# Two-layer hybrid block on one core: retention through a running state, norm factors spread by fp32r products, and side work started at other places

## The chip, the core and the metric

The kernel runs on one core of a Trainium2 chip. Its five engines are TensorE (PE, matrix products; PEld in the profile is its weight load), VectorE (DVE), ScalarE (ACT), GpSimd (POOL) and SyncE (SP, which here only issues DMAs). Each engine carries out its own instructions in the order in which the program lists them, and waits at an instruction until the data and buffers it needs are there. The metric is device time of one launch in microseconds (us); smaller is better.

## The reference, cut to what matters

Two layers, 512 tokens (S), width 1024 (D), four heads of 128 in each of three branches, feed-forward width 2816. Everything is float32.

```python
def retention(q, k, v):                      # CHUNK = 64
    q = rotary(q, pos); k = rotary(k, pos) * dk ** -0.5
    log_g = log1p(-exp2(-5.0 - arange(h)))   # one decay per head
    d_intra = exp(abs(idx[:, None] - idx[None, :]) * log_g)
    scores = einsum('bnihd,bnjhd->bnhij', qc, kc) * d_intra
    o_intra = einsum('bnhij,bnjhe->bnihe', scores, vc)
    kv = einsum('bnjhd,bnjhe->nbhde', kc * k_w, vc)
    _, r_prev = lax.scan(lambda r, kv_n: (g_chunk * r + kv_n, r), 0, kv)
    return o_intra + einsum('bnihd,nbhde->bnihe', qc * q_w, r_prev)

def hybrid_layer(x, ...):
    h = modulate(rms_norm(x, norm1_g), shift1, scale1)
    rq, rk, rv, rg, gq, gk, gv, glr, gg, fq, fk, fv, ff = split(h @ w_in)
    ret = silu(rg) * head_group_norm(retention(rq, rk, rv))
    gla_o = silu(gg) * rms_norm(gla(gq, gk, gv, log_a))
    fox_o = forgetting_attention(rms_norm(fq), rms_norm(fk), fv, ff + b_fox_f)
    mixed = sum(sigmoid(h @ w_mg + b_mg) * (branches @ w_br)) @ w_o
    x = x + gate1 * mixed
    h2 = modulate(rms_norm(x, norm2_g), shift2, scale2)
    u, g = split(h2 @ w_up)
    return x + gate2 * ((silu(causal_dwconv(u)) * g) @ w_down)
```

## The kernel before

**The big projections.** Activations lie as eight 128x512 tiles (`h[kc]`, features down the partitions, tokens along). Weights come in units of 128x1024. A unit is loaded by SP's queue (`wr`), its upper half is cast by ACT (`wh`, L175), the rest is subtracted by DVE (`wl`, L184), and every product is made of three one-pass fp32r products (`mm3`, L295 to L297: wh with hhi, wh with hlo, wl with hhi). `ahead()` prepares the units some steps ahead. A `col_block` is one output tile of 128x512: 8 x 3 = 24 such products. `head_group` (L428) is the first stage after a norm, where the inputs `h[kc]` are still being made: by `h_a` and `h_b` (DVE `ht`, ACT `hhi`, DVE `hlo`), tile by tile. At the start of the kernel it runs on eight banks with whole 512-column tiles. In the three later places (`half`: before layer 0's feed-forward, before layer 1's projections, before layer 1's feed-forward) it runs on six banks and takes each of its 8 tiles in two halves of 256 columns, so that the first half of the tokens starts before the norm of the second half is known.

**The norm.** `Norm.sums` (L346) makes the sum of squares per token by products with a column of ones (`nrm`), DVE makes v, POOL the power -1/2 (`r`, L352). `Norm.spread` (L354) multiplies r, broadcast, by the identity (float32, L356), which puts the factor of each token on all partitions (`nrmb`); ACT copies it to `rb`.

**After the head group of a layer.** The token group (L697 to L699, 276 columns; `tok_group`) makes the columns that are needed token by token. On ACT and DVE it is accompanied by `t_sum` and `t_low` (L598 to L617: sums and differences of the tiles of h for the paired projections, `ta`, `tb` and their casts `tah`, `tbh`, `tal`, `tbl`). Then the `col_block`s of the forgetting attention's q and k, the retention's v, the gates and so on follow.

**Side work.** What lies between the projections is written as generators: `qk_norm` (the norm of fq and fk: ACT squares `qsq` L544, cast `qsh`, DVE `qsl`, two products `qn` with ones L549 and L550), `gates_item` (forget gates: transposes, elementwise steps, a scan L741, transposes `cumc` L745, a DMA on POOL's queue), `la_item`, `fox_item` (L803, L819), `kv_item`, `ret_item`, `gla_item`. They wait in `queue` and are advanced by `tick()`, which each `col_block` calls twice. A tick lets every active item take one elementwise phase (`yield E_`) and then one phase on PE (`yield P1`, `P2`: with so many of the NA = 3 banks of the pool `psa`). An item in the queue starts when the counter `cool` has run down; each tick lowers it by one, and a started item sets it again by the second number with which it was queued. The order of all engines is thus fixed when the program is built.

**Retention.** Per head four items, `ret_item(hh, jb)`, one for each key block jb. Each makes the scores of its 128 keys against all later queries (L942: 512, 384, 256, 128 columns, float32), DVE multiplies by the decay table `dec` and PE adds up `ro` (L954, 1, 2, 3 and 4 products of 128 columns). The four decay tables are loaded by SP's queue at one place ahead of the first item. The four items of a head follow each other with `cool` 1.

**The start.** Ten warm-up products on the tile `warm` (W0), five (W1) and again ten (W2) fill PE while x, c and the first weights come in; between them the squares of x and the Silu of c are made.

A bank is a PSUM tile, and a slot is one of the NSLOT = 65 tiles of 128x512 that all side work shares.

Of the kernel before, what the change touches and what calls it, by code (L numbers as in the profile page):

```python
# [19 lines left out]
W0, W1, W2 = 10, 5, 10  # L20
# [6 lines left out]
NH = 4  # L27
# [19 lines left out]
for _n, _w in (("ident", 128), ("suf", 128), ("mask", 128), ("ind", 2),  # L47
               ("eps", 1), ("heps", 1), ("one", 1), ("mhalf", 1)):
    CC[_n] = (_o, _w)
    _o += _w  # L50
# [38 lines left out]
def tile_hybrid_layers(ctx: ExitStack, tc: tile.TileContext, xT, cvec, wall, wada, par, a2, cst, tabs, out):  # L89
# [45 lines left out]
    ones = const.tile([128, 128], F32, tag="ones", name="ones")  # L135
    onesr = const.tile([128, 128], F32R, tag="onesr", name="onesr")
# [200 lines left out]
    class Norm:  # L337
        def __init__(self, acc):
            self.acc = acc
            self.ps = bm("nrm")  # L340
            self.pb = bm("nrmb")
            self.rb = slot("rb")
            self.v = sm_p.tile([128, 4], F32, tag="v", name="v")
            self.r = sm_p.tile([128, 4], F32, tag="r", name="r")

        def sums(self, b0, b1):  # L346
# [5 lines left out]
            G.tensor_tensor(r, v, cc("mhalf").to_broadcast([128, b1 - b0]), op=ALU.pow)  # L352
# [60 lines left out]
    def head_group(l, sec, nm, h, half):  # L413
# [6 lines left out]
        def mms(kc, hf, bs=range(GB)):  # L420
# [5 lines left out]
            for n, (wi, hi) in enumerate(((0, 0), (1, 0), (0, 1))):  # L426
                for f in fl:
                    T.matmul(banks[f % GB][:, ts], lhsT=got[f // 8][wi][:, (f % 8) * 128:(f % 8) * 128 + 128],  # L428
                                 rhs=h[kc][hi][:, ts], start=kc == 0 and hf != 1 and n == 0,
                                 stop=kc == KD - 1 and n == 2, skip_group_check=hf is not None)  # L430
# [25 lines left out]
        else:  # L456
            hq = [(1, 0), (2, 0), (3, 0), (0, 1), (1, 1)]
            for kc in range(2, KD):
                hq += [(kc + 2, 0)] * (kc + 2 < KD) + [(kc, 1)]
            hp = []  # L460

            def hc(n=1):
                for _ in range(n):
                    if hq:
                        kc, hf = hq.pop(0)
                        hp.append((kc, hf, h_a(l, sec, kc, nm.rb, h, HS[hf])))
                    if hp and (len(hp) > 1 or not hq):
                        kc, hf, t = hp.pop(0)
                        h_b(l, sec, kc, t, h, HS[hf])
# [6 lines left out]
            hc()  # L476
# [5 lines left out]
            for kc in range(KD):  # L482
                hc()
                mms(kc, 1)
                hc()
                ahead()
                if kc + 3 < KD:
                    mms(kc + 3, 0)
# [48 lines left out]
    def layer(l, nm, h):  # L537
# [46 lines left out]
        cool[0] = 10 if l else 6  # L584
# [134 lines left out]
        def gates_item():  # L719
# [21 lines left out]
            V.tensor_tensor_scan(cum[0:4], e[0:4], m[0:4], 0.0, op0=ALU.mult, op1=ALU.add)  # L741
            yield P1
# [195 lines left out]
        def ret_item(hh, jb):  # L938
            w = S - jb * 128
            yield ("p", 1, lambda: [("rq", hh) in R, ("rk", hh) in R, ("rv", NB - 1) in R, ("dec", hh) in R])  # L940
            ps = ba("rs")
            T.matmul(ps[:, 0:w], lhsT=R["rk", hh][:, jb * 128:jb * 128 + 128], rhs=R["rq", hh][:, jb * 128:S],  # L942
                     start=True, stop=True)
# [5 lines left out]
            yield P0 if jb else P1
            if jb == 0:  # L950
                R["ro", hh] = ba("ro")
            po = R["ro", hh]
            for j in range(jb + 1):
                T.matmul(po[:, jb * 128:jb * 128 + 128],  # L954
                         lhsT=R["rP", hh, j][:, (jb - j) * 128:(jb - j) * 128 + 128],
                         rhs=R["rv", j][:, hh * 128:hh * 128 + 128], start=j == 0, stop=j == jb)
            if jb < NB - 1:
                return
# [59 lines left out]
        for i in range(4):  # L1018
            col_block(h, rot_evac("rk", i))
        for hh in range(NH):  # L1020
            R["dec", hh] = slot("dec")
            Q.dma_start(out=R["dec", hh], in_=tabs[2 + hh])
        for hh in range(NH):
            for jb in range(NB):
                queue.append((ret_item(hh, jb), 1))
# [174 lines left out]
    with tc.manual_schedule():  # L1200
# [20 lines left out]

        pc = [bm("cb"), bm("cb")]
# [184 lines left out]
```

## Time and profile before

| what | value |
|---|---|
| time, median of 3 runs | 1830.86 us (1830.72 to 1831.59) |
| the profiled execution, its time | 1827.52 us |
| its span, first to last instruction | 1825.8 us |
| mean granted TensorE clock | 0.996 |
| HBM read | 237.41 MB, 132 GB/s over the span |
| time of the packets of the hardware DMA queue, as a share of 16 engines' span | 36.1% |
| POOL busy | 128.4 us, 7% |
| ACT waiting for PE before a weight cast | 204.2 us in 62 waits |

A row of the timeline is: start, duration, engine, line, operation, output<-inputs, shapes, count; in brackets the idle time of the engine just before, and what ended it. A group row has busy time, mean duration in ns, then the idle time before its instructions. A row of the windows is: the stretch, its length, then busy time of PE, PEld, DVE, ACT and POOL with the counts, the granted clock of PE, the busy share of the DMA engines and their GB/s. Matmuls are pipelined and their ends are modelled, so the distance of two starts tells what a product costs, not its listed duration. A float32 product leaves two matmul records, an fp32r product and a transpose one.

### The profile page before, as it was taken

The page shows a single profiled execution, that of the slowest core. Times are in us where ns is not written, and L with a number is a line of the kernel's source. Part 1 is how long each engine was busy: PE and PEld are TensorE (multiplying, and loading weights), DVE is VectorE, ACT ScalarE, POOL GpSimd, SP SyncE. Part 2 cuts the span into 40 slices and gives each one's busy share as a digit, 9 for nine tenths or more (in the row PEclk, how much of TensorE's full clock was granted, in tenths as well). Part 3 has the DMA queues.
Part 4 walks back from the last instruction along what each step waited for, and adds up shares of the span by engine and source line. Part 5 has one row for each costly group of instructions (what it writes and reads, how often), then busy time and mean ns, then how long its engine had stood idle before and what let it go on. Part 6 is the DMA issues. An engine that isn't in the chain of part 4 may idle for free.

```text
span 1825.8 us, 22697 instructions
## 1 busy us (share of the span) xinstructions
PE 1786.8 (98%) x8895; PEld 1486.4 (81%) x8895; DVE 1059.9 (58%) x1643; ACT 715.8 (39%) x1192; POOL 128.4 (7%) x152
## 2 busy tenths in 40 slices
PE   9998999999999999999999989999999999999999
PEld 6776878888889888888898767788888898888887
DVE  7876674675666776754257767745444466445321
ACT  4577533432324433332146765334223244333220
POOL 3222010100000000000001210101000000000000
PEclk9999999999999999999999999999999999999999
DMA  9477332356452565554324762322422223232131
GB/s 358 127 170 174 104 104 81 127 185 221 160 173 93 166 217 198 199 196 166 98 76 108 204 152 80 116 69 76 144 93 92 81 93 115 93 103 94 47 124 48
DMA packets 72519, 243.11 MB, mean 133 GB/s; under 512 B 8232, under 2 KB 8658, under 8 KB 72412
## 3 DMA queue, kind: packets, MB, share of 16 engines
q1 hardware_dynamic: 66444, 220.67, 36.1%
q0 software_dynamic: 5968, 20.99, 5.9%
q8 instruction: 70, 1.15, 0.3%
q14 instruction: 37, 0.30, 0.1%
HBM read 237.41 MB, written 4.21 MB: 132 GB/s over the span
## 4 chain that ended last, share of the span: by engine, by line
PE 83%; DVE 8%; ACT 5%; issue 2%; POOL 1%; DMA 0%; SPq 0%; POOLq 0%; ACTq 0%; DVEq 0%
PE bm L295 22%; PE bm L297 22%; PE bm L296 22%; PE bm L428 4%; PE ga L428 4%; DVE wl L184 2%; ACT wh L175 2%; PE bm L647 1%; PE bm L651 1%; PE bm L649 1%; PE ro L954 1%; PE rs L942 1%; DVE fl L809 1%; DVE qsl L531 1%; POOL qsq L557 1%
## 5 line engine op out<-in xcount | busy, mean ns | idle before, releaser
L184 DVE TENSOR_TENSOR wl<-wr,wh 128x1024 fp32r<-128x1024 f32 x326 | 397.5, 1222 | 296.2 <-ACT wh L175 294.3
L295 PE MATMUL bm<-hhi,wh 128*128 128x512 f32 x1232 | 494.9, 402 | 0.0
L297 PE MATMUL bm<-hhi,wl 128*128 128x512 f32 x1232 | 480.9, 390 | 0.0
L296 PE MATMUL bm<-hlo,wh 128*128 128x512 f32 x1232 | 480.5, 390 | 0.0
L175 ACT CAST wh<-wr 128x1024 fp32r<-128x1024 f32 x326 | 338.6, 1046 | 304.1 <-PE bm L296 204.2
L295 PEld LDWEIGHTS bm<-hhi,wh 128*128 128x128 f32 x1232 | 231.7, 188 | 52.8 <-issue 5.3
L296 PEld LDWEIGHTS bm<-hlo,wh 128*128 128x128 f32 x1232 | 231.9, 188 | 50.6 <-issue 2.9
L297 PEld LDWEIGHTS bm<-hhi,wl 128*128 128x128 f32 x1232 | 231.7, 188 | 49.5
L295 PE MATMUL bm<-fah,wh 128*128 128x512 f32 (+1 forms) x374 | 141.0, 377 | 0.0
L296 PE MATMUL bm<-fal,wh 128*128 128x512 f32 (+1 forms) x374 | 140.8, 377 | 0.0
L297 PE MATMUL bm<-fah,wl 128*128 128x512 f32 (+1 forms) x374 | 140.8, 377 | 0.0
L205 DVE SCALAR_TENSOR_TENSOR ar<-ar,cact 128x1024 f32<-128x1024 f32 x80 | 97.4, 1217 | 0.0
L1090 DVE SCALAR_TENSOR_TENSOR x<-bm,mod,x 128x512 f32<-128x512 f32 (+1 forms) x39 | 25.5, 655 | 101.5 <-PE bm L297 101.5
L295 PEld LDWEIGHTS bm<-fah,wh 128*128 128x128 f32 x374 | 70.4, 188 | 13.0
L297 PEld LDWEIGHTS bm<-fah,wl 128*128 128x128 f32 x374 | 70.4, 188 | 13.0
L296 PEld LDWEIGHTS bm<-fal,wh 128*128 128x128 f32 x374 | 70.4, 188 | 12.7
L1127 ACT ACTIVATE fu<-fu 128x512 f32<-128x512 f32 x44 | 27.8, 632 | 102.9 <-DVE fu L1125 102.8
L1128 DVE TENSOR_TENSOR fu<-fu,bm 128x512 f32<-128x512 f32 x42 | 28.9, 688 | 65.3 <-PE bm L297 53.9
L334 ACT ACTIVATE sq<-x 128x512 f32<-128x512 f32 (+1 forms) x35 | 19.0, 545 | 104.1 <-DVE x L1090 103.0
L1050 ACT ACTIVATE mg<-bm,der 128x512 f32<-128x512 f32 x48 | 33.0, 688 | 65.2 <-PE bm L297 65.2
L295 PE MATMUL bm<-mxh,wh 128*128 128x256 f32 (+1 forms) x176 | 58.6, 333 | 0.0
L296 PE MATMUL bm<-mxl,wh 128*128 128x256 f32 (+1 forms) x176 | 58.3, 331 | 0.0
(256 smaller groups left out, 2718.6 us busy)
## 6 DMA issues: line engine op xcount, KB each, us to landing
wr<-wall SPq DMA_DIRECT2D x302, 512.0 KB, 3.8
ar<-wada SPq DMA_DIRECT2D x80, 512.0 KB, 4.7
wr<-wall POOLq DMA_DIRECT2D x32, 512.0 KB, 6.1
ad<-wada SPq DMA_DIRECT2D x32, 256.0 KB, 6.2
x<-xT SPq DMA_DIRECT2D x16, 256.0 KB, 4.8
cumb<-cumd POOLq DMA_DIRECT2D x8, 256.0 KB, 7.4
dec<-tabs SPq DMA_DIRECT2D x8, 256.0 KB, 2.7
x<-xs SPq DMA_DIRECT2D x8, 256.0 KB, 5.4
```

Source lines behind the costliest of these rows:

```text
L175: A.copy(hi, raw[plan[i][1]])
L184: V.tensor_tensor(lo, raw[plan[i][1]], hi.bitcast(F32), op=ALU.subtract)
L205: V.scalar_tensor_tensor(out=r, in0=r, scalar=1.0, in1=cact, op0=ALU.mult, op1=ALU.mult, accum_out=mod[l][:, b:b + 1])
L295: T.matmul(o, lhsT=wh, rhs=ah, start=first, stop=False)
L296: T.matmul(o, lhsT=wh, rhs=al, start=False, stop=False)
L297: T.matmul(o, lhsT=wl, rhs=ah, start=False, stop=last)
L334: A.activation(t[:, ts], x[k][:, ts], AF.Square)
L428: T.matmul(banks[f % GB][:, ts], lhsT=got[f // 8][wi][:, (f % 8) * 128:(f % 8) * 128 + 128], rhs=h[kc][hi][:, ts], start=kc == 0 and hf != ...
L1050: A.activation(g, o, AF.Tanh, scale=0.5, bias=der[l][:, i * 8 + j:i * 8 + j + 1])
L1090: V.scalar_tensor_tensor(out=x[j][:, ts], in0=o[:, ts], scalar=mod[l][:, sec * 8 + j:sec * 8 + j + 1], in1=x[j][:, ts], op0=ALU.mult, op1= ...
L1127: A.activation(t, t, AF.Silu)
L1128: V.tensor_tensor(t, t, pg, op=ALU.mult)
```

## The change

1. The warm-up at the start is shorter (W0 10 to 8, W2 10 to 4), and the two Silu of c come after all squares of x.
2. `Norm.spread`: r is split into rh and rl (two small DVE operations in `sums`), and two fp32r products with the identity take the place of one float32 product.
3. `head_group`, half form: the tiles 0 to 2 still go in halves, the tiles 3 to 7 as whole 512 columns.
4. `cool` after the head group is 4 (layer 0) and 8 (layer 1), before 6 and 10: `qk_norm` starts two ticks earlier.
5. `gates_item` has one more `yield E_` between the scan and its transposes.
6. Retention: one item per head. Scores within a block of 128 only (4 products of 128 columns), keys turned token by token (3 transposes, `rkT`), weighted by ACT with the column `kdec` (`rkw`), 3 products with v (`rkv`), a running state of three blocks (`rst`: one ACT copy, two DVE operations), queries times decay (`rqd`), and 4 + 3 products for `ro`. Items follow each other with `cool` 4. The decay tables are loaded one head at a time, in the item of the head before.
7. One slot fewer (64).

```diff
-W0, W1, W2 = 10, 5, 10
+W0, W1, W2 = 8, 5, 4
...
@@ Norm.sums
             G.tensor_tensor(r, v, cc("mhalf").to_broadcast([128, b1 - b0]), op=ALU.pow)
+            V.tensor_copy(self.rh[:, b0:b1], r)
+            V.tensor_tensor(self.rl[:, b0:b1], r, self.rh[:, b0:b1].bitcast(F32), op=ALU.subtract)
@@ Norm.spread
-                T.matmul(self.pb[:, b * 128:b * 128 + 128], lhsT=self.r[:, b:b + 1].to_broadcast([128, 128]),
-                         rhs=cc("ident"), start=True, stop=True)
+                T.matmul(o, lhsT=self.rh[:, b:b + 1].to_broadcast([128, 128]), rhs=identr, start=True, stop=False)
+                T.matmul(o, lhsT=self.rl[:, b:b + 1].to_broadcast([128, 128]), rhs=identr, start=False, stop=True)
@@ head_group, half
-            hq = [(1, 0), (2, 0), (3, 0), (0, 1), (1, 1)]
-            for kc in range(2, KD):
-                hq += [(kc + 2, 0)] * (kc + 2 < KD) + [(kc, 1)]
+            hq = [(1, 0), (2, 0), (0, 1), (1, 1), (2, 1)] + [(kc, None) for kc in range(3, KD)]
...
             for kc in range(KD):
                 hc()
-                mms(kc, 1)
-                hc()
+                mms(kc, 1 if kc < 3 else None)
                 ahead()
-                if kc + 3 < KD:
-                    mms(kc + 3, 0)
@@ layer
-        cool[0] = 10 if l else 6
+        cool[0] = 8 if l else 4
@@ gates_item
             V.tensor_tensor_scan(cum[0:4], e[0:4], m[0:4], 0.0, op0=ALU.mult, op1=ALU.add)
+            yield E_
             yield P1
             pc = ba("cumc")
@@ retention
-        def ret_item(hh, jb):
...
+        def ret_item(hh):
+            dec_load(hh + 1)
...
+            yield ("p", 2, lambda: [("rv", NB - 1) in R])
+            ps, pt = ba("rs"), ba("rkT")
+            for b in range(NB):
+                T.matmul(ps[:, bl(b)], lhsT=rk[:, bl(b)], rhs=rq[:, bl(b)], start=True, stop=True)
+            for b in range(NB - 1):
+                T.transpose(pt[:, bl(b)], in_=rk[:, bl(b)], identity=cc("ident"))
+            yield E_
+            kw, pm = slot("rkw"), slot("rP")
+            A.activation(kw[:, 0:384], pt[:, 0:384], AF.Copy, scale=C[:, o + hh:o + hh + 1])
+            V.tensor_tensor(pm.rearrange("p (a b) -> p a b", a=NB), ps.rearrange("p (a b) -> p a b", a=NB),
+                            dec[:, None, 0:128].to_broadcast([128, NB, 128]), op=ALU.mult)
+            free(2)
+            yield E_
+            qd = slot("rqd")
+            V.tensor_tensor(qd[:, 128:S], rq[:, 128:S], dec[:, 128:S], op=ALU.mult)
+            yield P1
+            pk = ba("rkv")
+            for b in range(NB - 1):
+                T.matmul(pk[:, bl(b)], lhsT=kw[:, bl(b)], rhs=R["rv", b][:, hs], start=True, stop=True)
+            yield E_
+            st = slot("rst")
+            A.copy(st[:, bl(0)], pk[:, bl(0)])
+            for b in range(1, NB - 1):
+                V.scalar_tensor_tensor(out=st[:, bl(b)], in0=st[:, bl(b - 1)], scalar=RG128[hh], in1=pk[:, bl(b)],
+                                       op0=ALU.mult, op1=ALU.add)
             free()
+            yield P1
+            po = ba("ro")
+            for b in range(NB):
+                T.matmul(po[:, bl(b)], lhsT=pm[:, bl(b)], rhs=R["rv", b][:, hs], start=True, stop=b == 0)
+                if b:
+                    T.matmul(po[:, bl(b)], lhsT=qd[:, bl(b)], rhs=st[:, bl(b - 1)], start=False, stop=True)
...
-                queue.append((ret_item(hh, jb), 1))
+            queue.append((ret_item(hh), 4))
@@ start
+        G.tensor_copy(identr, cc("ident"))
...
-            if k in (K0, K1):
-                i = int(k == K1)
-                A.activation(cact[:, i * S:i * S + S], pc[i], AF.Silu)
+        for i in range(2):
+            A.activation(cact[:, i * S:i * S + S], pc[i], AF.Silu)
-NSLOT = 65
+NSLOT = 64
```

What edit 4 does to the order of PE in layer 0 shows at the end of the token group. Before, the first norm products come 24 products behind it:

```order
L697 MATMUL bm<-wh,hhi 128x276
L698 MATMUL bm<-wl,hhi 128x276
L699 MATMUL bm<-wh,hlo 128x276
L295 MATMUL bm<-hhi,wh 128x512
...
L297 MATMUL bm<-hhi,wl 128x512
L549 MATMUL qn<-qsh,onesr 128x512
L550 MATMUL qn<-qsl,onesr 128x512
L295 MATMUL bm<-hhi,wh 128x512
```

Of the change, at the same place:

```order
L700 MATMUL bm<-wh,hhi 128x276
L701 MATMUL bm<-wl,hhi 128x276
L702 MATMUL bm<-wh,hlo 128x276
L552 MATMUL qn<-qsh,onesr 128x512
L553 MATMUL qn<-qsl,onesr 128x512
L296 MATMUL bm<-hhi,wh 128x512
L297 MATMUL bm<-hlo,wh 128x512
```

The two `qn` products now stand right behind the token group; all other products of this stage keep their order. Layer 1 has the same picture.

On ACT, in the token group of layer 0, the square and the cast that feed these products stood so before, up to the first `qsh`:

```order
L608 CAST tbh<-tb 128x512
L175 CAST wh<-wr 128x1024
L606 CAST tah<-ta 128x256
L607 ACTIVATE tah<-ta,tabd 128x256
L608 CAST tbh<-tb 128x512
L544 ACTIVATE qsq<-qk 128x512
L175 CAST wh<-wr 128x1024
L530 CAST qsh<-qsq 128x512
```

and stand so in the change, from the same `tbh` on:

```order
L611 CAST tbh<-tb 128x512
L547 ACTIVATE qsq<-qk 128x512
L176 CAST wh<-wr 128x1024
L609 CAST tah<-ta 128x256
L610 ACTIVATE tah<-ta,tabd 128x256
L611 CAST tbh<-tb 128x512
L533 CAST qsh<-qsq 128x512
L547 ACTIVATE qsq<-qk 128x512
L176 CAST wh<-wr 128x1024
```

The first square moved up by one step of the token group, and the first cast `qsh` now stands where the first square stood: behind the cast `tbh` of the third tile.

On PE, among the retention's products in layer 0, before (a part of the first head):

```order
L297 MATMUL bm<-hhi,wl 128x512
L942 MATMUL rs<-rq,rk 128x384
L295 MATMUL bm<-hhi,wh 128x512
...
L297 MATMUL bm<-hhi,wl 128x512
L954 MATMUL ro<-pr,rP 128x128
L942 MATMUL rs<-rq,rk 128x256
L295 MATMUL bm<-hhi,wh 128x512
```

and in the change (scores of the first head, and further on its outputs):

```order
L298 MATMUL bm<-hhi,wl 128x512
L958 MATMUL rs<-rq,rk 128x128 x4
L960 MATMUL rkT<-cst,rk 128x128 x3
L296 MATMUL bm<-hhi,wh 128x512
...
L298 MATMUL bm<-hhi,wl 128x512
L985 MATMUL ro<-pr,rP 128x128 x2
L987 MATMUL ro<-rst,rqd 128x128
L985 MATMUL ro<-pr,rP 128x128
L987 MATMUL ro<-rst,rqd 128x128
L985 MATMUL ro<-pr,rP 128x128
L987 MATMUL ro<-rst,rqd 128x128
```

The retention's products come in fewer and larger pieces between the same projection products; between the scores and the outputs of a head now lie three steps on ACT and DVE and the `rkv` products.

More of the change, by code (lines that the diff above doesn't have):

```diff
@@ L47 @@
 for _n, _w in (("ident", 128), ("suf", 128), ("mask", 128), ("ind", 2),
-               ("eps", 1), ("heps", 1), ("one", 1), ("mhalf", 1)):
+               ("eps", 1), ("heps", 1), ("one", 1), ("mhalf", 1), ("kdec", 4)):
     CC[_n] = (_o, _w)
@@ L135, in tile_hybrid_layers @@
     ones = const.tile([128, 128], F32, tag="ones", name="ones")
+    identr = const.tile([128, 128], F32R, tag="identr", name="identr")
     onesr = const.tile([128, 128], F32R, tag="onesr", name="onesr")
@@ L344, in __init__ @@
             self.r = sm_p.tile([128, 4], F32, tag="r", name="r")
+            self.rh = sm_p.tile([128, 4], F32R, tag="rh", name="rh")
+            self.rl = sm_p.tile([128, 4], F32R, tag="rl", name="rl")
         def sums(self, b0, b1):
@@ L429, in mms @@
                                  rhs=h[kc][hi][:, ts], start=kc == 0 and hf != 1 and n == 0,
-                                 stop=kc == KD - 1 and n == 2, skip_group_check=hf is not None)
+                                 stop=kc == KD - 1 and n == 2, skip_group_check=half)
         if not half:
@@ L456, in head_group, with hs @@
         else:
-            hq = [(1, 0), (2, 0), (3, 0), (0, 1), (1, 1)]
-            for kc in range(2, KD):
-                hq += [(kc + 2, 0)] * (kc + 2 < KD) + [(kc, 1)]
+            hq = [(1, 0), (2, 0), (0, 1), (1, 1), (2, 1)] + [(kc, None) for kc in range(3, KD)]
             hp = []
+            def hs(hf):
+                return FULL if hf is None else HS[hf]
             def hc(n=1):
@@ L483, in head_group @@
                 hc()
-                mms(kc, 1)
-                hc()
+                mms(kc, 1 if kc < 3 else None)
                 ahead()
-                if kc + 3 < KD:
-                    mms(kc + 3, 0)
         depth[0] = 4
@@ L936, in gla_item, with dec_load @@
             yield from head_out(1, hh, os, st[:, 4:8], None, der[l][:, 28:29], R["gg", hh])
-        def ret_item(hh, jb):
[L939 to L943, printed above, removed]
-            yield E_
-            pt = slot("rP")
-            V.tensor_tensor(pt[:, 0:w], ps[:, 0:w], R["dec", hh][:, 0:w], op=ALU.mult)
-            R["rP", hh, jb] = pt
-            free()
[L949 to L958, printed above, removed]
+        def dec_load(hh):
+            if hh < NH:
+                R["dec", hh] = slot("dec")
+                Q.dma_start(out=R["dec", hh], in_=tabs[2 + hh])
@@ new lines, in ret_item, with bl @@
+        def ret_item(hh):
+            dec_load(hh + 1)
+            hs = slice(hh * 128, hh * 128 + 128)
+            rq, rk, dec = R["rq", hh], R["rk", hh], R["dec", hh]
+            def bl(b):
+                return slice(b * 128, b * 128 + 128)
+            yield ("p", 2, lambda: [("rv", NB - 1) in R])
[4 more added lines that the diff above has]
+                T.transpose(pt[:, bl(b)], in_=rk[:, bl(b)], identity=cc("ident"))
+            yield E_
+            kw, pm = slot("rkw"), slot("rP")
+            o, _ = CC["kdec"]
+            A.activation(kw[:, 0:384], pt[:, 0:384], AF.Copy, scale=C[:, o + hh:o + hh + 1])
[15 more added lines that the diff above has]
+                                       op0=ALU.mult, op1=ALU.add)
+            free()
+            yield P1
[4 more added lines that the diff above has]
+                    T.matmul(po[:, bl(b)], lhsT=qd[:, bl(b)], rhs=st[:, bl(b - 1)], start=False, stop=True)
@@ L1019, in layer @@
             col_block(h, rot_evac("rk", i))
+        dec_load(0)
         for hh in range(NH):
[L1021 to L1024, printed above, removed]
-                queue.append((ret_item(hh, jb), 1))
+            queue.append((ret_item(hh), 4))
         for i in range(4):
@@ L1241, in tile_hybrid_layers @@
             nm, h = layer(l, nm, h)
-NSLOT = 65
 DBG = 0
+RG128 = [(1.0 - 2.0 ** (-5 - hh)) ** 128 for hh in range(NH)]
+NSLOT = 64
 def _layout(inputs):
@@ L1384, in _layout @@
         tabs[2 + hh] = dec * float(HD) ** -0.5
+        tabs[2 + hh][:, 128:] = np.exp((np.arange(S)[None, 128:] % 128 + 1) * lg[hh])
+        cst[:, CC["kdec"][0] + hh] = np.exp((127 - np.arange(128)) * lg[hh]) * float(HD) ** -0.5
     return {
```

5 lines of the change are left out of this document (3 added, 2 removed).

## The prediction

> **What bounds the kernel now.** I read the page's busy times first, then the chain that ended last.
>
> ```profile
> span 1825.8 us, 22697 instructions
> PE 1786.8 (98%) x8895; PEld 1486.4 (81%) x8895; DVE 1059.9 (58%) x1643; ACT 715.8 (39%) x1192; POOL 128.4 (7%) x152
> PE 83%; DVE 8%; ACT 5%; issue 2%; POOL 1%; DMA 0%; SPq 0%; POOLq 0%; ACTq 0%; DVEq 0%
> ```
>
> PE is busy 98% of the span. So the time changes only by what PE executes, by the holes in it, and by its clock. The holes are 1825.8 - 1786.8 = 39 us. DVE and ACT count only at the few places where the chain leaves PE (13%). The program's time was 1827.52 in this execution; the median of the runs is 1830.86, 3.34 more. I work against the execution and add 3.34 at the end.
>
> **Retention: PE work removed.** Timeline of PE in layer 0, one product group of the outputs, then one of the scores; the two group rows by shape; a window in which these stages run; the loads of the decay tables.
>
> ```profile
> 293.43 1.05 PE L954 MATMUL ro<-pr,rP 128*128 128x128 f32 x8
> 294.32 0.81 PE L942 MATMUL rs<-rq,rk 128*128 128x384 f32 x2
> 295.20 0.40 PE L296 MATMUL bm<-hlo,wh 128*128 128x512 f32 x1
> L954 PE MATMUL ro<-pr,rP 128*128 128x128 f32 x160 | 23.0, 274 | 0.0
> L903 PE MATMUL oT<-cst,ros 128*128 128x128 f32 x32 | 4.8, 272 | 0.0
> 300.00:320.00 20.00, 20.00 (x102) 16.48 (x101) 10.77 (x24) 8.15 (x23) 1.54 (x2) 1.00 0.33 106
> dec<-tabs SPq DMA_DIRECT2D x8, 256.0 KB, 2.7
> ```
>
> Eight records take 294.32 - 293.43 = 0.89, 0.111 each. L954's 160 records are 80 products, so a float32 product of 128 columns is two records, 0.222. The 32 transposes of L903 are one record each: 0.111. The score of 384 columns takes 295.20 - 294.32 less one projection product (0.227, below) = 0.65, or 1.7 ns a column; by that 512 columns cost 0.865, 256 cost 0.435. Before, a head costs 0.865 + 0.65 + 0.435 + 0.222 for scores and 10 x 0.222 for outputs: 4.39. After: 4 scores, 3 `rkv`, 7 outputs, 14 x 0.222, and 3 transposes at 0.111: 3.44; I count the saving as 0.96. Eight heads: **-7.7**. The new steps on ACT (`rkw`, a copy) and DVE (`rP`, `rqd`, two state steps) lie beside PE: in the window DVE is busy 10.77 of 20 us, ACT 8.15, PE has no hole, and between a head's scores, `rkv` and outputs the program puts 24 and more projection products (over 5 us). So I price the new waits at 0; if that cover is gone they cost what rival D says. A table needs 2.7 us and is issued one head ahead, over 36 products (8 us): 0 on SP's queue, though it stands behind weight loads there.
>
> **Head groups: whole tiles.** Two pairs of rows: halves in layer 1, whole tiles in layer 0.
>
> ```profile
> 935.22 0.52 PE L428 MATMUL ga<-hhi,wh 128*128 128x256 f32 x3
> 935.58 0.52 PE L428 MATMUL bm<-hhi,wh 128*128 128x256 f32 x3
> 22.31 0.84 PE L428 MATMUL ga<-hlo,wh 128*128 128x512 f32 x3
> 22.99 1.30 PE L428 MATMUL bm<-hlo,wh 128*128 128x512 f32 x5
> 24.12 0.39 PE L428 MATMUL ga<-hhi,wh 128*128 128x512 f32 x1
> ```
>
> Three halves take 0.36, 0.120 each; eight whole ones (24.12 - 22.31) take 1.81, 0.2265 each. A tile of 6 banks is 36 x 0.120 = 4.32 in halves and 18 x 0.2265 = 4.08 whole: 0.24 less. Five tiles, three places: **-3.6**. The weight units and `h` must then be ready in whole tiles; rival B takes this back.
>
> **The scan's transposes.** The group row, and two windows in layer 0, around the wait and behind it.
>
> ```profile
> L745 PE MATMUL cumc<-cst,cum 4*128 4x4 f32 x8 | 0.8, 197 | 4.0 <-DVE cum L741 4.0
> 115.15:118.55 3.40, 1.44 (x9) 1.27 (x10) 3.28 (x4) 1.57 (x3) 0.56 (x1) 1.00 0.71 136
> 118.57:121.96 3.39, 3.39 (x10) 2.16 (x8) 3.39 (x6) 1.53 (x2) 1.21 (x3) 0.50 0.52 161
> ```
>
> PE waits 4.0 us for the scan, in the two layers together. With a step between, another tick's products (12 or more, over 2.7 us) cover it; what was queued behind, the next projection products, starts earlier. And the window behind the wait has a granted clock of 0.50: half of its 3.39 us is lost, 1.6 to 1.7. Together **-5.6**. If the scan is later still, the wait comes back; I see no reason, since DVE starts it at the same point.
>
> The Trainium skill, TensorE: Matmul & The Clock Gate, section "Part 1: The HAM clock gate", says that the clock falls to half after at least one idle window of about 3.4 us. By that rule a wait of 2 us gives no half rate, the term would be -4.0 instead of -5.6. The windows quoted here and below speak against it: 1.44, 1.50 and 1.67 us of PE in 3.4 were enough, each time the next window had 0.50.
>
> **The earlier norm products: a new wait.** Timeline of layer 0 with all engines, the two windows there; then layer 1; then the last pair of layer 0.
>
> ```profile
> 74.52 0.40 PE L295 MATMUL bm<-hhi,wh 128*128 128x512 f32 x1
> 79.41 0.62 ACT L608 CAST tbh<-tb 128x512 fp32r<-128x512 f32 x1 [0.68 <-DVE tb L604]
> 79.94 0.62 ACT L544 ACTIVATE qsq<-qk 128x512 f32<-128x512 f32 x1
> 81.41 0.61 ACT L530 CAST qsh<-qsq 128x512 fp32r<-128x512 f32 x1
> 82.07 0.49 PE L549 MATMUL qn<-qsh,onesr 128*128 128x512 f32 x1 [1.90 <-ACT qsh L530]
> 82.67 0.68 DVE L531 TENSOR_TENSOR qsl<-qsq,qsh 128x512 fp32r<-128x512 f32 x1
> 83.41 0.50 PE L550 MATMUL qn<-qsl,onesr 128*128 128x512 f32 x1 [0.84 <-DVE qsl L531]
> 83.75 0.39 PE L295 MATMUL bm<-hhi,wh 128*128 128x512 f32 x1
> 81.01:84.42 3.41, 1.50 (x5) 1.05 (x6) 2.85 (x9) 2.98 (x8) 0.00 (x0) 1.00 0.00 0
> 84.43:87.83 3.40, 3.40 (x9) 2.67 (x8) 3.06 (x8) 2.66 (x6) 0.00 (x0) 0.50 0.01 2
> 979.86 0.40 PE L295 MATMUL bm<-hhi,wh 128*128 128x512 f32 x1
> 982.96 0.63 ACT L544 ACTIVATE qsq<-qk 128x512 f32<-128x512 f32 x1
> 986.44 0.50 PE L550 MATMUL qn<-qsl,onesr 128*128 128x512 f32 x1 [0.71 <-DVE qsl L531]
> 992.37:995.77 3.40, 1.67 (x7) 1.13 (x7) 2.53 (x3) 3.40 (x7) 1.66 (x2) 1.00 0.71 105
> 995.79:999.19 3.40, 3.40 (x10) 2.63 (x9) 2.22 (x5) 2.64 (x5) 1.16 (x1) 0.50 0.25 49
> 158.00 0.50 PE L549 MATMUL qn<-qsh,onesr 128*128 128x512 f32 x1 [0.40 <-ACT qsh L530]
> 159.57 0.50 PE L550 MATMUL qn<-qsl,onesr 128*128 128x512 f32 x1 [1.07 <-DVE qsl L531]
> ```
>
> Before, PE leaves the token group at 74.52, has 24 products (24 x 0.2265, to 79.96), should be over the pair at 80.41 and goes on at 83.75: 3.3 lost, and 1.7 by half rate. After, PE wants the pair at 74.52. In ACT's order `qsh` now takes the place of `qsq`, behind the `tbh` that waits for DVE's `tb` until 79.41; the square, put ahead of a weight cast, pushes all that by about 0.5. So `qsh` runs from some 80.5 to 81.1, `qsl` to 81.9, and PE goes on at 82.15: 82.15 - 74.52 - 0.45 = 7.2 lost. A window mostly idle lies behind, so the clock is at half until the window ends at 84.43: 1.1 more. That is 8.3 against 5.0, +3.3 (if the half rate lasted a whole window, +0.6 on top). Of the next three pairs one finds its whole chain late (about 2.0, as the pair at 158.00 does: 0.40 + 1.57 - 0.23 and the start-up) where two now wait for `qsl` alone: +1.1. The last pair of the layer, 2.0, comes a step earlier, behind elements that are done: -2.0. Layer 0: **+2.5**.
>
> Layer 1: PE is there at 979.86, `qsh` takes the place at 982.96 plus 0.5 and ends at 984.1, the second product about 0.8 later, PE goes on near 985.1: 4.8 and half rate 1.7. Before, its first two pairs lost 1.0 and 2.2, and 1.7 at half rate (995.79); after, the two behind the first wait some 1.2 and 0.5. 8.2 against 4.9, less the last pair's 2.0: **+1.4**, rounded with layer 0 to **+4.0**.
>
> **The rest.** The wait for slots, the first POOL power, the forget branch:
>
> ```profile
> ACT fah L530 <- PE bm L296: 14.2, 2, 7.1
> L352 POOL TENSOR_TENSOR r<-v,cst x7: 695/695/1621, 13.4 to 1462.5; 128x2 f32<-128x2 f32 x6, 128x4 f32<-128x4 f32 x1
> L803 PE MATMUL fs<-qk 128*128 128x512 f32 x16 | 8.6, 619 | 3.7 <-ACT fpT L822 3.7
> L819 PE MATMUL fT<-cst,fl 128*128 128x128 f32 x80 | 14.5, 279 | 3.9 <-ACT fpT L822 2.3 <-ACT fl L815 1.3
> ```
>
> Spreading by fp32r: 16 products of 128 columns at 0.222 become 32. If each cost as much as a transpose, 0.111, nothing changes; if half of a 256-column one, 0.060, -1.6. I take 0, nearer the transpose, which has the same width, and keep -0.8 and +0.3. The new `rl` waits for POOL's r (0.695, once 1.621), and DVE in order behind it: at the later norms DVE has products ahead of it to hide behind, and one wait of about 0.2 goes (**-0.2**). At the start DVE's first `ht` comes 0.3 to 1.1 later, and six warm-up products fewer let PE take it at once: 0, with -0.7 and +1.7 as ends. The forget branch as a whole moves 24 products ahead; its 3.7 and 3.9 us of waits may halve or grow by half: 0, ends -4 and +4. One slot fewer: ACT waited 7.1 us for one, but there with PE busy, and weights are prepared four units ahead: 0.
>
> **The sum.** -7.7 - 3.6 - 5.6 + 4.0 - 0.2 = -13.1; 1827.52 becomes 1814.4, and with 3.34 on top **1817.8**. Own range, from the ends of the rest: 1813 to 1823.
>
> **Rivals.**
> - A: the early pairs don't wait. ACT gets square and cast done ahead of `tbh`. Then +4.0 falls away and the last pairs' 2.0 each stay saved: 1817.8 - 8.0 = 1809.8. For it: ACT is idle 0.68 ahead of `tbh`. Against: its order has `qsh` behind it.
> - B: whole tiles are later than halves. DVE makes each in one piece, PE waits for it, 0.24 a tile is eaten: 1817.8 + 3.6 = 1821.4. For it: the chain leaves PE for ACT and DVE at 13%. Against: a tile gives PE 4.1 us.
> - C, slower: all early pairs wait, not the first alone. The pairs behind the first (three in each layer, six) also find ACT and DVE late, because the square and cast of each now stand ahead of the weight casts and delay `tb`. Each at layer 1's price of 4.8 + 1.7 instead of the 1.2 or so in my sum gives 6 x 5.3 = 32: 1850. It decides from (1830.86 - 1817.8 + 3.7) / 6 = 2.8 a pair. Against: 18 to 24 products lie between two pairs.
> - D: the state form does not pay. Its chain (scores, DVE, `rkv`, ACT and DVE state, outputs) makes PE wait 0.96 a head: 1817.8 + 7.7 = 1825.5. Against: no hole in the window at 300.
> - E: partial waits were not what halved the clock, and removing the scan's wait brings 4.0 only: 1819.4. Against: three windows above. (This is what the skill's rule would make of it.)
>
> **How the numbers follow.** Forecast 0.55, A 0.15, B 0.10, D 0.08, C 0.05, E 0.03, something unseen 0.04. About 0.2%, 3.7 us, is what a measurement of this kernel can tell from no change, so faster means under 1827.2. The forecast, A, B, E and most of D are: 0.90. Same 0.04 (the rest of D and of the unseen), slower 0.06 (C and some unseen). The range reaches to A and to just short of D: 1808 to 1825.
>
> **What would show it.** In the profile of the changed kernel: no idle time at the `cumc` transposes, and no window at 0.50 behind them; `qn` waiting about 6.6 us right behind the token group of layer 0, and 4 in layer 1, then 0.50; L954's place taken by products whose sum is about 8 us less, with no idle time at `ro` and `rkv`; five tiles of each later head group in 18 records with starts 0.227 apart. A wait of PE at `rkv` or `ro`, or at whole tiles of the head group, or at several `qn` pairs of 3 us or more, would make the prediction wrong.

## The result, and the profile after

| | before | changed |
|---|---|---|
| median of the runs | 1830.79 us (4 runs, 1830.12 to 1831.59) | 1815.95 us (4 runs, 1815.21 to 1817.87) |
| the profiled execution | 1827.52 us | 1816.21 us |

The ratio is 0.992, with a 95% interval of 0.9903 to 0.9938: 14.8 us faster, where 13.1 was forecast (1817.8, range 1808 to 1825). (Before has one run more here than ahead of the prediction, hence 1830.79 for 1830.86.) The two profiled executions lie 11.3 apart, since that of before was 3.3 below its median and that of the change is an ordinary one.

The page of the changed kernel: span, busy times, chain.

```profile
span 1814.4 us, 22215 instructions
PE 1774.4 (98%) x8641; PEld 1473.4 (81%) x8641; DVE 1056.3 (58%) x1627; ACT 717.3 (40%) x1193; POOL 127.3 (7%) x153
PE 86%; DVE 6%; ACT 4%; issue 2%; POOL 1%; DMA 0%; SPq 0%; DVEq 0%; POOLq 0%; ACTq 0%
```

PE has 254 records fewer and 12.4 us less busy time; its holes are 40 us as before (39). So the work that left PE paid, and the waits changed places. What PE waited for shows in the view of the waits (engine, tile, line <- who ended the wait: us in all, times, longest). Before:

```profile
PE qn L550 <- DVE qsl L531: 9.1, 11, 1.1
PE qn L549 <- ACT qsh L530: 5.2, 8, 1.9
PE fs L803 <- DVE fl L807: 4.3, 4, 1.2
PE cumc L745 <- DVE cum L741: 4.0, 2, 2.0
PE fs L803 <- ACT fpT L822: 3.7, 4, 1.0
PE fT L819 <- ACT fpT L822: 2.3, 2, 1.2
PE fT L819 <- ACT fl L815: 1.3, 2, 0.6
```

The changed kernel:

```profile
PE qn L552 <- ACT qsh L533: 12.4, 6, 6.4
PE fs L807 <- ACT fpT L826: 6.6, 7, 1.6
PE qn L553 <- DVE qsl L534: 6.6, 9, 1.0
PE bm L296 <- ACT mg L1076: 3.6, 2, 1.8
PE fs L807 <- DVE fl L811: 1.8, 2, 0.9
```

The scan's wait (4.0) is gone. The norm pairs wait 19.0 instead of 14.3, the forget branch (`fs`, `fT`) 8.4 instead of 11.6. And one wait is new: 3.6 us for `mg`, in two pieces.

To see where the time went, I cut PE's timeline at the first product of each head group and at the first one behind it:

| stage | before, us | changed, us | difference |
|---|---|---|---|
| up to layer 0's first head group | 18.45 | 18.92 | +0.5 |
| layer 0, from there to the head group of its feed-forward | 538.51 | 535.47 | -3.0 |
| that head group | 35.68 | 34.68 | -1.0 |
| layer 0's feed-forward | 328.50 | 328.15 | -0.35 |
| layer 1's first head group | 35.68 | 34.66 | -1.0 |
| layer 1, to the head group of its feed-forward | 502.49 | 497.16 | -5.3 |
| that head group | 35.68 | 34.69 | -1.0 |
| the rest | 326.20 | 326.18 | 0 |

The starts sum to -11.3. Within the two long stages I took the distances of the starts around each block of side work, less 0.227 for each projection product (so the launch of a product after a wait counts too, and numbers are a little above the idle times):

| side work, both layers | before | changed | difference |
|---|---|---|---|
| retention, linear attention, transposes of their outputs | 55.3 | 52.2 | -3.1, of it -7.3 work and +4.2 the wait for `mg` |
| forget branch | 64.6 | 58.9 | -5.7 |
| norm pairs of q and k (with one transpose block) | 28.5 | 33.1 | +4.6 |
| scan's transposes and the gates' products beside them | 17.6 | 12.6 | -4.9 |
| projection products at half clock | 4.6 | 6.4 | +1.8 |

With the stages outside (-3.0 head groups, -0.35, +0.5) this gives -10.2 of the -11.3; 1.1 lies in distances of some ns that I don't assign.

### The profile page after: what moved, and what is told of

It reads as the page before. It is cut to its first block, busy times and chain, and to the rows that moved or that the text cites. A ratio compares the mean times of both kernels' runs of the same rounds, so it can differ in the third digit from the quotient of the medians.

```text
span 1814.4 us, 22215 instructions
## 1 busy us (share of the span) xinstructions
PE 1774.4 (98%) x8641; PEld 1473.4 (81%) x8641; DVE 1056.3 (58%) x1627; ACT 717.3 (40%) x1193; POOL 127.3 (7%) x153
## 4 chain that ended last, share of the span: by engine, by line
PE 86%; DVE 6%; ACT 4%; issue 2%; POOL 1%; DMA 0%; SPq 0%; DVEq 0%; POOLq 0%; ACTq 0%
PE bm L296 23%; PE bm L298 23%; PE bm L297 22%; PE bm L434 4%; PE ga L434 4%; DVE wl L185 2%; PE bm L650 2%; PE bm L654 1%; PE bm L652 1%; ACT wh L176 1%; PE fs L807 1%; DVE fl L813 1%; PE fo L833 1%; DVE qsl L534 0%; DVE fl L811 0%
## 5 line engine op out<-in xcount | busy, mean ns | idle before, releaser
L534 DVE TENSOR_TENSOR fal<-fu,fah 128x512 fp32r<-128x512 f32 x44 | 30.5, 693 | 61.1 <-PE bm L297 32.2
L1076 ACT ACTIVATE mg<-bm,der 128x512 f32<-128x512 f32 x48 | 33.1, 690 | 73.6 <-PE bm L298 70.8
```

The source lines that it names most:

```text
L534: V.tensor_tensor(lo, src, hi.bitcast(F32), op=ALU.subtract)
L1076: A.activation(g, o, AF.Tanh, scale=0.5, bias=der[l][:, i * 8 + j:i * 8 + j + 1])
```

## The experiments

All are timed against the kernel before on the same chip.

| kernel | median, us | before beside it | ratio (95%) |
|---|---|---|---|
| changed | 1815.95 | 1830.79 | 0.992 (0.9903 to 0.9938) |
| 1 changed, evacuations ahead of the tick | 1810.15 | 1830.47 | 0.9888 (0.9871 to 0.9904) |
| 2 changed, float32 spread | 1817.73 | 1830.47 | 0.9932 (0.9914 to 0.9951) |
| 3 as 2, old start of the norm of q and k | 1814.10 | 1830.47 | 0.9911 (0.9896 to 0.9925) |
| 4 before, retention alone | 1824.34 | 1830.47 | 0.9969 (0.9957 to 0.998) |
| 5 as 3, evacuations ahead | 1812.37 | 1829.19 | 0.9912 (0.9897 to 0.9927) |
| 6 as 1, norm start half way | 1817.15 | 1829.19 | 0.9939 (0.9924 to 0.9954) |
| 7 before, step behind the scan alone | 1822.30 | 1829.19 | 0.9962 (0.9948 to 0.9976) |
| 8 before, whole tiles alone | 1826.78 | 1829.19 | 0.9987 (0.9978 to 0.9996) |
| 9 as 1, a step ahead of the norm pairs | 1805.86 | 1830.06 | 0.9866 (0.9851 to 0.9881) |
| 10 before, earlier norm start alone | 1835.78 | 1830.06 | 1.0029 (1.0019 to 1.0038) |
| 11 as 9, all evacuations ahead of side work | 1822.25 | 1829.88 | 0.996 (0.9944 to 0.9975) |
| 12 changed, old start of the kernel | 1816.71 | 1829.88 | 0.9928 (0.9916 to 0.994) |

**1. The new wait for `mg`.** First the timeline of the changed kernel at that place, PE and ACT:

```profile
333.82 0.39 PE L298 MATMUL bm<-fbh,wl 128*128 128x512 f32 x1
334.05 0.60 PE L985 MATMUL ro<-pr,rP 128*128 128x128 f32 x4
...
335.81 0.28 ACT L992 ACTIVATE ros<-ro 128x128 f32<-128x128 f32 x1 [5.18 <-PE ro L987]
...
336.83 0.71 ACT L1076 ACTIVATE mg<-bm,der 128x512 f32<-128x512 f32 x1
337.58 0.50 PE L296 MATMUL bm<-hhi,wh 128*128 128x512 f32 x1 [1.81 <-ACT mg L1076]
```

The chain goes round: PE makes the outputs `ro` of the last head, ACT had waited 5.18 us for them to read them out (`ros`, four operations), behind them in ACT's order stands `mg`, whose bank PE needs for its next product. ACT could have done `mg` long ago (kernel 1 below does it at 322.52); it stood behind an instruction that waited for PE. Two windows there show what follows:

```profile
334.90:338.31 3.41, 1.60 (x11) 1.31 (x11) 0.69 (x1) 1.72 (x9) 0.00 (x0) 1.00 0.30 113
338.31:341.72 3.41, 3.41 (x11) 2.65 (x10) 0.00 (x0) 0.00 (x0) 0.00 (x0) 0.55 0.00 0
```

PE was busy 1.60 of 3.41 us, and the next window has a clock of 0.55. The edit (`flush()` issues the evacuations that wait, `mg` among them, and `tick` the side work):

```diff
                     if jj:
+                        flush()
                         tick(1, False)
```

> The changed kernel, with the waiting evacuations issued ahead of the tick in the branch products. Theory: in the changed kernel PE waits twice (once a layer, 1.81 us of idle time, 2.1 by starts) for ACT's mg, because the four ros reads of the last retention head, which wait for PE itself, stand ahead of mg on ACT; in layer 0 a stretch at half clock follows (8 products, some 1.7 us). Put ahead, mg frees the bank in time: 2 x 2.1 + 1.7 = 5.9 less than the changed kernel, about 1810. Rival: the bank is late for another reason (the weight units or DVE's mix behind it), and the wait only gets another releaser: 1816.

Measured: 1810.15, and no `mg` among PE's waits. The theory's 1810 was met; the new wait and the half clock behind it cost 5.8 us of the change's gain. The stretch at half clock behind this place is gone from its trace as well.

**2 and 3. Spread, and the start of the norm of q and k.** Kernel 2 puts back the float32 product in `Norm.spread` and 65 slots. Kernel 3 has that and

```diff
-        cool[0] = 8 if l else 4
+        cool[0] = 10 if l else 6
```

> The changed kernel with the norm factors spread by float32 products again (and 65 slots). Theory: 16 products of two records against 32 of one, equal cost, so no difference in the trace at nrmb: 1816 within 1; the first DVE operation of the start may come 0.3 to 1 earlier. Rival: float32 costs four passes and the fp32r form saved up to 1.6: 1817.6.

> As the kernel with the float32 spread and 65 slots, and the norm of q and k started at the ticks of before (cool 6 and 10). Theory: the wait of 6.4 and 4.1 us at the first pair goes and the pairs cost 4.6 less by starts, but the forget branch stands 24 products later again and loses its 5.7: net +1, about 1817. Rival: the forget branch's gain has nothing to do with that shift (it came with the step behind the scan), then only the 4.6 are saved: about 1811.5.

Kernel 2 came to 1817.73, with runs from 1814.71 to 1822.42: by time alone the rival's 1817.6 can't be told from no difference. The trace is clearer, PE at the second norm of layer 0, of before and of the changed kernel:

```profile
561.96 0.60 PE L356 MATMUL nrmb<-cst,r 128*128 128x128 f32 x4
562.32 0.37 PE L428 MATMUL ga<-hhi,wh 128*128 128x256 f32 x1
```

```profile
559.42 0.22 PE L362 MATMUL nrmb<-identr,rh 128*128 128x128 f32 x1
559.48 0.27 PE L363 MATMUL nrmb<-identr,rl 128*128 128x128 f32 x1
559.59 0.28 PE L362 MATMUL nrmb<-identr,rh 128*128 128x128 f32 x1
559.70 0.28 PE L363 MATMUL nrmb<-identr,rl 128*128 128x128 f32 x1
559.82 0.45 PE L434 MATMUL ga<-hhi,wh 128*128 128x256 f32 x2
```

Two blocks of 128 tokens take 0.36 by float32 and 0.40 by four fp32r products; an fp32r product of 128 columns takes 0.11, as much as one of the two records of a float32 one. Nothing was to be won there. Kernel 3 came to 1814.10. Its waits show both halves of the theory: `qn` waits 9.6 and 5.2 us again as before, the forget branch 4.3, 3.8, 2.3 and 1.3, and its blocks cost 32.3 and 32.4 us in the two layers as before (changed: 29.1 and 29.8). So the forget branch's gain does come from the shift, and is about given back by the first pairs. The total is 1.9 below the changed kernel, not 1 above, and 3.6 below kernel 2, from which it differs by this edit alone; but the intervals of the ratios overlap, so the medians don't decide whether the earlier start helps or harms the whole change. The theory left out that the wait for `mg` is smaller there (1.9 instead of 3.6) and that its trace has one stretch at half clock behind the start, where the changed kernel has four.

**4. Retention alone.** The kernel before with the state form (edit 6 of the change).

> The kernel before with the retention in state form alone. Theory: -7.7 of PE work, and the wait for mg of 2.1 a layer appears here too, with or without a stretch at half clock (1.7): 1830.8 - 7.7 + 4.2 = 1827.3, or 1829 with it. Rival: the wait for mg comes from the other shifts, then 1823. Second rival: the state form's steps make PE wait at rkv or ro, then at 1831.

Measured: 1824.34, 6.1 less. PE's waits of this kernel, the new row:

```profile
PE bm L295 <- ACT mg L1075: 1.9, 2, 0.9
```

No `rkv` and no `ro` is among them. The wait for `mg` appears here too, but half as long, and behind another read-out: ACT's row just ahead of this `mg` is not `ros` but the copy `rst`, which waits for the products `rkv`.

```profile
338.10 0.27 ACT L976 COPY rst<-rkv 128x128 f32<-128x128 f32 x1 [1.90 <-PE rkv L973]
```

So the result lies between theory and rival: -7.5 of work (below) and about +2.5.

**5 and 6. Other starts of the norm of q and k, without the wait for `mg`.** Kernel 5 is kernel 3 with the edit of experiment 1, kernel 6 is kernel 1 with `cool` 5 and 9.

> The changed kernel with both: evacuations issued ahead of the tick in the branch products, and the norm of q and k at the ticks of before (with the float32 spread and 65 slots). Theory: against the kernel with the old ticks (1814.1), the two waits behind ros of 1.3 by starts go: 1811.5. So the old ticks and the new ones are within 2 of each other once the wait for mg is out. Rival: the old ticks are better by themselves by what the medians of the two earlier runs differ (3.6): 1806.5.

> The changed kernel with the evacuations issued ahead of the tick, and the norm of q and k started one tick earlier than before (cool 5 and 9, where before has 6 and 10 and the change 4 and 8). Theory: the first pair stands 12 products behind the token group, which cover 2.7 of its wait in each layer, and the forget branch keeps its gain, if what gains is that it no longer runs beside the last norm pairs: 1810.15 - 5.4 = 1804.7. Rival: the forget branch's waits depend on the half step (which products lie between two of its steps): half or all of its 5.8 comes back, 1808 to 1810.5.

Kernel 5: 1812.37, 2.2 above kernel 1 (near the 1811.5 of the theory). The two waits for `mg` that it removes stood behind `rst`, as in experiment 4, not behind `ros`. Kernel 6: 1817.15, a miss, 7 above kernel 1. (Beside these two, before came to 1829.19, beside kernel 1 to 1830.47; by the ratios they lie 4.4 and 9.3 above it.) Its first pair does wait less (3.8 at most), but `qsh` now ends a wait of PE 11 times, not 6 (12.4 us in all), `qsl` 12 times (9.9 us), and `fl` costs the transposes of the forget branch 4.6. The pairs stand 18 to 24 projection products apart, as in kernel 1; why more of them wait at the half step isn't shown.

**7 and 8. The scan's step, and the whole tiles, alone.**

> The kernel before with the extra step between the scan and its transposes alone. Theory: the wait of 2.17 a layer goes (4.3 to 4.9) and the half clock behind the one in layer 0 (1.4): 1830.6 - 6 = 1824.6. Rival: half rate has nothing to do with these partial waits, then 1826; second rival: the forget branch starts later or otherwise by that step and its waits change by a few us, either way, with fox waits not at 8.8 a layer.

> The kernel before with whole tiles 3 to 7 in the three later head groups alone. Theory: 5 tiles x 3 x 0.24 = 3.6 less: 1827.0. Rival: DVE's whole tiles are later and PE waits in the head groups: 1830.6.

Kernel 7: 1822.30, 6.9 less, by the interval 4.4 to 9.5. The group row shows the wait gone:

```profile
L749 PE MATMUL cumc<-cst,cum 4*128 4x4 f32 x8 | 0.8, 204 | 0.0
```

In its trace no stretch at half clock follows at 118, where before had one, and the forget branch costs 32.3 us a layer as before: this edit doesn't touch it. The stretch at 995.8 is missing too (one stretch is left, three stood before), so not all of the 6.9 need be the wait and the half clock behind it. Kernel 8: 1826.78, 2.4 less (0.7 to 4.0), the 3.6 of the theory within the interval and the rival's 0 outside it. The changed kernel's rows at a whole tile in layer 1 are

```profile
935.56 0.84 PE L434 MATMUL ga<-hhi,wh 128*128 128x512 f32 x3
936.24 0.84 PE L434 MATMUL bm<-hhi,wh 128*128 128x512 f32 x3
936.92 0.84 PE L434 MATMUL ga<-hhi,wl 128*128 128x512 f32 x3
```

three products each 0.68, 0.227 each, without idle time between.

**9 and 10. A step ahead of the norm pairs; the earlier start alone.** Kernel 9 is kernel 1 with

```diff
             sh, sl = split(sq, "qs")
+            yield E_
             yield P1
...
-        cool[0] = 8 if l else 4
+        cool[0] = 7 if l else 3
```

Kernel 10 is the kernel before with `cool` 4 and 8.

> The kernel with the evacuations ahead of the tick (1810.15), and in the norm of q and k one more step between the cast and its two products, started one tick earlier (cool 3 and 7), so that PE's order stays and the square and cast stand one step further ahead on ACT. Theory: the pairs wait because cast and products belong to one tick, as the scan and its transposes did; the first cast then stands behind the second tile's tbh (74.6 to 75.2 in the profile of before), qsh is ready at some 76.4, the first pair costs 3 instead of 7.2 in layer 0 and 1 instead of 4.8 in layer 1, and the later pairs lose most of their 2.0: 12 to 18 less, 1792 to 1798. Rival: ACT and DVE bound this stage, and what the pairs no longer wait the weight products or the forget branch wait instead: 1807 or more.

> The kernel before with the earlier start of the norm of q and k alone (cool 4 and 8). Theory: the waits of the first pairs appear (6.4 and 4.1 us), the pairs cost 4 to 5 more by starts, the forget branch 5.8 less, half clock as before: 1829 to 1831, no change that can be told. Rival: the forget branch's gain needs the extra step behind the scan as well, then it is 5 slower, 1835.

Kernel 9 is the fastest of all: 1805.86, 10 below the changed kernel and 24 below before. But it gained 4.3, not 12 to 18. Its group rows at the pairs, and the waits that took their place:

```profile
L554 PE MATMUL qn<-qsl,onesr 128*128 128x512 f32 x16 | 6.8, 424 | 0.4 <-DVE qsl L534 0.4
L553 PE MATMUL qn<-qsh,onesr 128*128 128x512 f32 x16 | 6.5, 409 | 2.7 <-ACT qsh L533 1.7 <-ACT qv L558 0.9
```

```profile
PE bm L296 <- DVE sml L716: 6.1, 2, 3.1
PE fT L824 <- ACT fl L820: 5.5, 4, 1.7
PE la L772 <- issue: 3.9, 2, 2.0
```

The pairs wait 3.1 us instead of the 18.0 of kernel 1, as the theory says, and 15.5 stand in three other places, of which kernel 1 has none. By starts, kernel 9 against kernel 1: the pairs with what follows them cost 13.0 less, the forget branch 4.6 less, the gates' products (`la`) 5.3 more, and the stretches at half clock 8.5 instead of 3.3, 5.2 more. (Together 7.1 less, where the spans of the two profiles differ by 5.0; how blocks that hold several kinds of work are shared out moves these parts by 1 to 2 us.) So the rival was right in part: the work of ACT and DVE in this stage wasn't reduced, only its order changed, and what they were late with next took over a good part of the wait.

Kernel 10 is slower than before by 5.7 us (3.5 to 7.0 by the interval), where I expected no change. The pairs cost 4.5 more by starts and the forget branch 5.0 less, as expected. Missed was the wait for `mg`: with the old retention too, PE waits 3.7 us (1.9 a layer) for it, 4.3 by starts, and its trace has five stretches at half clock behind the start where before has three. ACT and PE there:

```profile
343.65 0.28 ACT L966 ACTIVATE ros<-ro 128x128 f32<-128x128 f32 x1 [4.53 <-PE ro L957]
345.42 0.50 PE L295 MATMUL bm<-hhi,wh 128*128 128x512 f32 x1 [1.87 <-ACT mg L1053]
```

This is the chain of experiment 1, with the old retention and as long as in the changed kernel (1.87 and 1.81). So the shift by 24 products alone brings the whole wait for `mg`; the new form alone brings half of one, behind `rst`. It depends on what ACT has in hand when the branch products need the bank.

**11. All evacuations ahead of side work.**

```diff
+        if fl:
+            flush()
         advance("e")
-        if fl:
-            flush()
         advance("p")
```

> The kernel with the extra norm step (1805.86), and every tick issues the waiting evacuations ahead of the elementwise steps of the side work, not behind them. Theory: PE there waits 3.1 us a layer behind the token group for the evacuation sml, which DVE can't do until ACT has copied gk, and ACT has five steps of the norm ahead of that copy; put ahead, the 6.1 go: 1799.7, or 1801 with other evacuations now delaying side work. Rival: the side work's steps, each an evacuation later, make PE wait elsewhere (fl, fpT of the forget branch) by as much: 1806.

Measured: 1822.25, 16 slower than kernel 9, worse than the rival. The wait for `sml` fell from 6.1 to 1.1, but the waits in the forget branch and at the norm pairs grew; of PE's waits:

```profile
PE qn L553 <- ACT qsh L533: 7.4, 3, 2.9
PE fT L824 <- ACT fl L820: 6.0, 4, 1.7
PE fs L808 <- DVE fl L812: 3.8, 2, 1.9
PE fT L824 <- DVE st L892: 3.6, 2, 1.8
```

By starts the forget branch's waits rose from 4.2 to 12.1 us in layer 0 and from 4.2 to 10.9 in layer 1: its steps, each behind an evacuation more, became the late ones. The norm pairs wait 10.6 us in all again (7.4 for `qsh`, 3.2 for `qsl`), where kernel 9 has 3.1.

**12. The old start of the kernel.**

> The changed kernel with the start of before (10, 5 and 10 warm-up products, each Silu between the squares). Theory: the start costs 0 to 0.5 either way (PE's first product of the head group at 18.5 in the profile of before, 18.9 in the changed one): 1815.5 to 1816. Rival: the rl split behind POOL delays the first tile, and six warm-up products more make PE take it later yet: 1817 or more.

Measured: 1816.71 (1815.61 to 1816.84), within the scatter of the changed kernel's 1815.95. Edit 1 is worth nothing that can be told.

## Why the prediction was right, point by point

- **What bounds the kernel.** Right: PE stays at 98%, and the gain is what its work lost.
- **Retention, -7.7.** Right as to work: by the starts a head cost 4.40 before (0.656 + 0.672 + 1.529 + 1.546 for its four blocks) and 3.47 after (1.231 + 0.671 + 1.565): 0.94 less, 7.5 in all (7.3 in the table by blocks). Rival D, a wait at `rkv` or `ro`, didn't occur; both have 0.0 idle time in their rows:

```profile
L985 PE MATMUL ro<-pr,rP 128*128 128x128 f32 x64 | 11.0, 274 | 0.0
L987 PE MATMUL ro<-rst,rqd 128*128 128x128 f32 x48 | 9.3, 275 | 0.0
L974 PE MATMUL rkv<-pr,rkw 128*128 128x128 f32 x48 | 6.6, 274 | 0.0
```

- **The step that failed** is "So I price the new waits at 0", and with it that the shift of edit 4 was priced at the norm pairs and the forget branch alone. I looked at what waits for the moved steps on PE, and not at what stands behind them on ACT: the read-outs `ros`, which wait for PE, had `mg` behind them. That cost 5.8 us with the half clock (experiment 1). The wait comes whole with the shift alone (1.87 us of idle time a layer, experiment 10) and half with the new form alone (0.94, experiment 4); in the changed kernel, which has both, it is 1.81.
- **Head groups, -3.6.** Right in kind: 1.0 a place by the stage table, 3.0 in all, against 1.2 a place predicted.
- **The scan's transposes, -5.6.** Right: the wait is 0.0, the blocks cost 4.9 less by starts, and the stretch at half clock behind it is gone. Experiment 7 measures 6.9 for this edit alone.
- **Half clock after partial waits.** Rival E is out. A further window, in the changed kernel, busy 1.60 of 3.41 us, is again followed by 0.55 (experiment 1), and the stretch behind the scan's wait is gone from the traces of the changed kernel and of kernel 7; it is there in kernels 4, 8 and 10, which keep that wait. The Trainium skill, TensorE: Matmul & The Clock Gate, section "Part 1: The HAM clock gate", asks for at least one idle window; the traces differ from it, and the measurement decides.
- **The earlier norm products, +4.0.** The waits of the first pairs came where and as long as worked out; the changed kernel, layer 0 and layer 1:

```profile
81.53 0.80 PE L552 MATMUL qn<-qsh,onesr 128*128 128x512 f32 x1 [6.44 <-ACT qsh L533]
...
979.18 0.50 PE L552 MATMUL qn<-qsh,onesr 128*128 128x512 f32 x1 [4.13 <-ACT qsh L533]
```

  6.44 where about 6.6 was written, 4.13 where 4 was. By starts the pairs cost 4.6 more. Rival A is out, and so is C: no later pair waits 2.8 more.
- **Forget branch, 0 with ends -4 and +4.** Mis-sized: -5.7, outside the ends. Experiment 3 shows that it comes from the shift by 24 products; experiment 10 finds it with the shift alone. Why its steps are less late there, the runs don't settle.
- **Spread, start, slot: 0.** Right within what could be told (2 and 12).
- **The sum.** For the execution 1814.4 was predicted, 1816.21 measured. Against the terms: the new wait +4.2; half clock +4.0 (2.2 less was written in the terms, 1.8 more was measured, since stretches came at 154 and at 338); whole tiles +0.6; start +0.5; retention's work +0.4 (the table's -7.3); layer 0's feed-forward -0.2; the scan's wait -0.9; the forget branch -5.7; and -1.1 not assigned. So two misses nearly cancel: the waits and half clock that were left out, and the forget branch. (The terms themselves come out a little otherwise when worked again, 0.95 a head for 0.96 and +3.7 for +4.0 at the pairs; the sum would be -13.3 for -13.1.) The 3.34 added on top was wrong for the changed kernel, whose profiled execution is 0.26 above its median. So 1817.8 is near 1815.95 because two errors went opposite ways: the execution was predicted 1.8 too fast, and the offset 3.6 too large. The terms for the work, the first pairs and the scan were understood; that the total is so near is luck.

Taken alone, retention gives -6.1, the scan's step -6.9, the whole tiles -2.4 and the earlier norm start +5.7. That makes -9.7, and the whole change gives -14.8. Of the difference 2.6 is the wait for `mg`, which experiments 4 and 10 both hold (2.5 and 4.3 by starts) and the change has once (4.2); the rest lies within the intervals of the four. The best version that ran keeps all edits, adds the earlier evacuation and the step ahead of the norm pairs: 1805.86.

## What to carry to other kernels

Where an engine's cast and the product that reads it belong to the same step of a hand-made order, PE waits for the whole chain; one step between them removes the wait, and what it uncovers is the next late step, so its price has to be looked up at the waits that stand beside it. When work is moved to another engine, ask not only who waits for it, but what stands behind it in that engine's order and who needs that: an evacuation that frees a PSUM bank should not stand behind a read-out that waits for PE. That is no rule for every place: put ahead at one place it gained 5.8 us (experiment 1), put ahead everywhere it cost 16 (experiment 11). And test each start time by itself: here one of seven edits cost 5.7 us alone, and the whole was still faster.

## What the runs showed of the hardware

Half clock does not need an idle window: windows of 3.4 us with PE busy 1.44 to 1.67 us were each followed by one at 0.50 to 0.55. In the changed kernel a window with no product at all is followed by half clock as well, and the one after that, behind a window busy 1.10 us, again. But the busy time of one window doesn't settle it: in layer 1 a window busy 1.52 us was followed by one at full clock, and only the next one, busy 0.91 us, by half clock, while a window busy 1.86 us, in layer 0, was followed by half clock.

```profile
75.82:79.23 3.41, 0.00 (x0) 0.00 (x0) 2.56 (x5) 1.73 (x4) 0.00 (x0) 1.00 0.97 215
79.23:82.64 3.41, 1.10 (x2) 0.63 (x3) 2.98 (x7) 2.73 (x5) 0.00 (x0) 0.50 0.03 7
82.64:86.06 3.42, 3.42 (x9) 2.65 (x9) 1.23 (x1) 3.21 (x7) 0.40 (x1) 0.50 0.02 5
150.91:154.32 3.41, 1.86 (x8) 1.04 (x8) 2.35 (x2) 2.53 (x4) 1.27 (x1) 1.00 0.88 153
154.33:157.74 3.41, 3.41 (x10) 2.62 (x9) 3.31 (x7) 1.34 (x3) 2.66 (x3) 0.50 0.33 49
973.52:976.93 3.41, 1.52 (x13) 1.30 (x11) 2.55 (x5) 1.73 (x4) 0.00 (x0) 1.00 0.16 66
976.94:980.35 3.41, 0.91 (x3) 0.55 (x4) 2.92 (x7) 2.73 (x5) 0.00 (x0) 1.00 0.00 0
980.35:983.76 3.41, 3.41 (x10) 2.67 (x9) 1.51 (x2) 3.38 (x8) 0.74 (x1) 0.50 0.00 0
```

The number of such stretches behind the start differs between kernels with nearly the same waits (one in experiment 7's trace, three in experiment 8's), each worth 1.3 to 2.7 us. How a wait falls into the windows has a part in it. In layer 1 PE waits about 2.0 us for the scan in the kernel before and in kernel 8 alike. Before, the window from 1019.68 to 1023.09 is busy 2.09 us and full clock follows; in kernel 8 the window from 1016.79 to 1020.20 is busy 1.37 us and half clock follows.

Whether this is what spreads the runs of one kernel over some us wasn't tested. Over the 109 runs of the experiments, each kernel against its own mean, time and mean granted clock go together only weakly (correlation -0.43).
